# Transpose banks at the start, the last waits, and the semaphores of an RMSNorm and matrix product

## The chip, the core and the metric

The kernel runs on one core of a Trainium2 chip. The time is the device time of one execution in microseconds (us). The core has five engines that run in parallel, each with an instruction stream of its own: TensorE (PE in the profile, with its weight loads as PEld), VectorE (DVE), ScalarE (ACT), GpSimd (POOL) and SyncE (SP). Sixteen DMA engines move data between the device memory (HBM) and the on-chip memory. Engines wait for each other, and for transfers, on semaphores.

## The reference

```python
batch, seq, dim, out_dim = 16, 1024, 512, 768
rms = np.sqrt(np.mean(x ** 2, axis=-1, keepdims=True) + eps)
x_norm = x / rms * gamma
return np.matmul(x_norm, weight).astype(np.float32)
```

There are 16384 rows of 512 numbers. Each is divided by its root mean square, multiplied by `gamma`, and multiplied by a 512 x 768 matrix. Input, weights and output are 32-bit floats: 33.6 MB of x are read and 50.3 MB of output are written.

## The kernel before

The rows are cut into 128 tiles of 128 rows, and two tiles make a pair `j`. The scale by the root mean square is put behind the product, since it is one number per row; `gamma` is multiplied into the weights once, which are kept as bfloat16.

For one tile, GpSimd casts x to bfloat16 (`cast`, L178). Two neighbouring bfloat16 numbers are taken as one 32-bit word, and TensorE turns blocks of 128 x 128 words (`transpose_word`, L216): two words' blocks per tile. They go to one of two PSUM banks, `tp[j % 2]`, so that both tiles of a pair share a bank. VectorE copies them to `xT` (`evac`, L224), for one tile at a time in pairs 0, 1 and 2 (pair 0 by `transpose_tile`, pairs 1 and 2 with `alone=True`) and for a whole pair afterwards. Four weight loads (`hold`, L281) and eight products (`product`, L285) per tile sum up in one of three accumulators `ops`. ScalarE scales the even tile of a pair and VectorE the odd one into the output buffer `ot` (`finish_tile`, `scale`, L264 and L266). ScalarE also computes the squares (L186) and the roots (L191), VectorE the reciprocals (L193). In some pairs VectorE turns the data instead of TensorE (`cast_quad`, `move`, L245 and L256).

SP issues the transfers of x, the weights and the output (L167, L328, L278), all on one queue, in the order in which they stand in the program. x is loaded in groups that begin small (2, 2, 4, 8 tiles), and the output is stored in groups (2, 2, 4, 4, 4, then 8 tiles, and 4 and 4 at the end). `ot` has three buffers of 8 tiles and `xt` two of 16, so a load can be issued when the buffer's tiles have been used.

Nothing is scheduled by a planner: the order on each engine is the order of the calls in the program. The class `Order` records each operation with the cells that it reads and writes, and `emit` then issues all of them and puts in the waits that the cells ask for. For each engine it keeps what the engine is known to have awaited, so that no wait is put in twice. An engine that waits stands still, with all that is queued behind it. In `emit`, an engine that others wait for has one counting semaphore. Each transfer that is awaited has one of its own, and at the end, at L87 and L88, SP waits for those transfers that nobody else awaits: the last four stores.

The recording is emitted within one `tile_critical` section. At its end SP releases a semaphore, each engine answers, SP waits for the answers, and then all engines meet at a barrier, GpSimd clears the program's semaphores in one instruction, and they meet once more.

The start, to which the change goes, is this order on TensorE (`warm_up(n)` is one weight load and `n` products of zeros that nothing uses):

```python
    warm_up(6)
    ...   # gamma is turned and copied, casts 0 to 3, norms 0 and 1
    warm_up(4)
    transpose_tile(0)
    transpose_tile(1)
    warm_up(2)
    weights(0, DVE, 0, WIDE)
```

Of the kernel before, what the change touches and what calls it, by code (L numbers as in the profile page):

```python
# [12 lines left out]
BF16 = mybir.dt.bfloat16  # L13
# [3 lines left out]
P = 128  # L17
# [3 lines left out]
class Order:  # L21
# [4 lines left out]

    def __init__(self, tc):
        self.tc, self.ops = tc, []  # L30

# [6 lines left out]
    def emit(self):  # L38
        nc = self.tc.nc
        streams = {id(e): n for n, e in enumerate((nc.tensor, nc.vector, nc.scalar, nc.gpsimd, nc.sync))}  # L40
        writer, readers = {}, {}
        known = [dict() for _ in streams]
        clocks, needs, place = [], [], []
        count = [0] * len(streams)
        for n, (proc, engine, _, reads, writes) in enumerate(self.ops):
            at = streams[id(engine)]
            if proc is None:
                me, turn = ("transfer", n), 1
            else:
                count[at] += 1  # L50
                me, turn = at, count[at]
            written = {writer[cell] for cell in reads + writes if cell in writer}
            read = {d for cell in writes for d in readers.get(cell, ())}
            need = []
            for d in sorted(written | read, reverse=True):
                who, when = place[d]
                if who == me and (engine is nc.tensor or d not in written):
                    continue
                if known[at].get(who, 0) < when:
                    need.append(d)  # L60
                    for k, v in clocks[d].items():
                        known[at][k] = max(known[at].get(k, 0), v)
            clock = dict(known[at])
            clock[me] = turn
            place.append((me, turn))
            clocks.append(clock)
            needs.append(need)
            for cell in reads:
                readers.setdefault(cell, []).append(n)
            for cell in writes:  # L70
                writer[cell], readers[cell] = n, []
        awaited = {d for need in needs for d in need}
        last = [n for n, (me, _) in enumerate(place) if not isinstance(me, int) and n not in awaited]
        sems, marks, done = {}, {}, {}
        for n in sorted(awaited | set(last)):
            me = place[n][0]
            if me not in sems:
                sems[me] = self.tc.alloc_semaphore(f"done{len(sems)}")
            done[me] = done.get(me, 0) + (1 if isinstance(me, int) else 16)
            marks[n] = (sems[me], done[me])  # L80
        for n, (proc, engine, issue, _, _) in enumerate(self.ops):
            for d in needs[n]:
                engine.wait_ge(*marks[d])
            ins = issue()
            if n in marks:
                ins.then_inc(marks[n][0], 1 if isinstance(place[n][0], int) else 16)
        for n in last:  # L87
            nc.sync.wait_ge(*marks[n])  # L88


@with_exitstack
def kernel(
# [8 lines left out]
    nc = tc.nc  # L101
    PE, DVE, ACT, POOL, SP = nc.tensor, nc.vector, nc.scalar, nc.gpsimd, nc.sync
    order = Order(tc)

    def run(engine, issue, reads=(), writes=()):
        order.add(1, engine, issue, reads, writes)

    x = x.flatten_outer_dims()
    out = out.flatten_outer_dims()
# [5 lines left out]
    XG, OG = 16, 8  # L115
    AHEAD = 20

    def stretches(group, parts):
        first, size, i = {}, {}, 0
        for g in range(NT // group):  # L120
            for n in parts.get(g, [group]):
                for t in range(i, i + n):
                    first[t], size[t] = i, n
                i += n
        return first, size

    last = NT // OG - 1
    x_first, x_size = stretches(XG, {0: [2, 2, 4, 8], **{g: [8, 8] for g in (1, 2, 5, 6, 7)}})
    o_first, o_size = stretches(OG, {0: [2, 2, 4], 1: [4, 4], last: [4, 4]})
# [5 lines left out]
    def sb(name, shape, dtype):  # L135
        return nc.alloc_sbuf_tensor(name, shape, dtype).ap()
# [6 lines left out]
    ident_f = sb("ident_f", [P, P], F32)  # L143
    g_sb = sb("g_sb", [P, 2, 2], F32)
    xt = [sb(f"xt{n}", [P, XG, D], F32) for n in range(2)]
    xb = [sb(f"xb{n}", [P, 8, D], BF16) for n in range(2)]
    jk = [sb(f"jk{n}", [P, D], BF16) for n in range(2)]
    xT = [sb(f"xT{n}", [P, 2, 2, P, 2], BF16) for n in range(4)]
    xq = [sb(f"xq{n}", [P, 4, D], BF16) for n in range(2)]
    xTq = [sb(f"xTq{n}", [P, 4, 2, P, 2], BF16) for n in range(2)]  # L150
    ot = [sb(f"ot{n}", [P, OG, O], F32) for n in range(3)]
    ssq = sb("ssq", [P, NT], F32)
    rms = sb("rms", [P, NT], F32)
    rstd = sb("rstd", [P, NT], F32)
    psum = nc.alloc_psum_tensor("ps", [P, 8 * WIDE], F32).ap()
    ops = [psum[:, 2 * WIDE * n:2 * WIDE * (n + 1)] for n in range(3)]
    tp = [psum[:, WIDE * n:WIDE * (n + 1)].rearrange("p (t h m) -> p t h m", t=2, h=2) for n in (6, 7)]

    def cells(name, slot, i, n=1):
        return [(name, slot, t) for t in range(i, i + n)]  # L160
# [28 lines left out]
    def root(i, n):  # L189
        s = slice(i, i + n)  # L190
        run(ACT, lambda: ACT.activation(out=rms[:, s], in_=ssq[:, s], func=AF.Sqrt, scale=1.0 / D, bias=eps_sb),  # L191
            [("ssq", t) for t in range(i, i + n)] + ["eps"], [("rms", i)])
        run(DVE, lambda: DVE.reciprocal(out=rstd[:, s], in_=rms[:, s]), [("rms", i)],  # L193
            [("rstd", t) for t in range(i, i + n)])

    def norms(i, n):
        for t in range(n):
            square(i + t)
        root(i, n)
# [6 lines left out]
    def norms_of_group(j):  # L206
        square(2 * j)
        square(2 * j + 1)
        if j in norm_end:
            root(*norm_end[j])  # L210

    def transpose_word(j, t, h):
        s = j // 4 % 2
        words = xb[s].rearrange("p a d -> p (a d)").bitcast(F32)
        lo = (j % 4 * 2 + t) * (D // 2) + h * P
        run(PE, lambda: PE.transpose(out=tp[j % 2][:, t, h, :], in_=words[:, lo:lo + P], identity=ident_f),  # L216
            cells("xb", s, j % 4 * 2 + t) + ["ident"], [("tp", j % 2)])

    xT_of = {}

    def evac(j, t=0, n=2):
        src = tp[j % 2].rearrange("p t h m -> p t (h m)").bitcast(BF16)
        dst = xT[j % 4].rearrange("p t h m c -> p t (h m c)")
        run(DVE, lambda: DVE.tensor_copy(out=dst[:, t:t + n, :], in_=src[:, t:t + n, :]),  # L224
            [("tp", j % 2)], cells("xT", j % 4, t, n))
        for a in range(t, t + n):
            xT_of[2 * j + a] = (xT[j % 4][:, a], ("xT", j % 4, a))

    def transpose_tile(i):
        for h in range(2):  # L230
            transpose_word(i // 2, i % 2, h)
        evac(i // 2, i % 2, 1)
# [29 lines left out]
    def scale(engine, dst, src, r, reads, writes):  # L262
        if engine is ACT:
            run(ACT, lambda: ACT.mul(out=dst, in_=src, mul=r), reads, writes)  # L264
        else:
            run(DVE, lambda: DVE.tensor_single_scalar(out=dst, in_=src, scalar=r, op=mybir.AluOpType.mult), reads, writes)  # L266
# [3 lines left out]
    def accumulator():  # L270
        return next(turns) % 3

    def store(i):
        first, n = o_first[i], o_size[i]
        s = first // OG % 3
        if i == first + n - 1:
            src = ot[s][:, first % OG:first % OG + n, :]
            order.transfer(SP, lambda: SP.dma_start(out=rows(out, first, n), in_=src), reads=cells("ot", s, first % OG, n))  # L278

    def hold(lhsT, cell):  # L280
        run(PE, lambda: PE.ldweights(lhsT), [cell])  # L281

    def product(dst, lhsT, rhs, start, stop, reads, writes):

        run(PE, lambda: PE.add_instruction(mybir.InstMatmult(  # L285
            name=nc.get_next_instruction_name(), engine=mybir.EngineType.PE,
            ins=[PE.lower_ap(rhs), PE.lower_ap(lhsT)], outs=[PE.lower_ap(dst)],
            start_tensor_calc=start, stop_tensor_calc=stop, tile_size=(P, P), tile_position=(0, 0), ldweights=False)),
            reads, writes)
# [11 lines left out]

    def finish_tile(i, a, engine):
        s = i // OG % 3
        scale(engine, ot[s][:, i % OG, :], ops[a][:, :O], rstd[:, i:i + 1],
              [("ops", a, 0), ("ops", a, 1), ("rstd", i)], [("ot", s, i % OG)])
        store(i)

    def feeder(pairs, gaps, alone=False):
# [34 lines left out]
    def warm_up(n):  # L343
        hold(warm[:, :P], "warm")
        for _ in range(n):
            product(ops[spare][:, :WIDE], warm[:, :P], warm, True, True, ["warm"], [("ops", spare, 0)])
# [15 lines left out]
    cast(1)  # L362
    cast(2, 2)
    norms(0, 2)
    warm_up(4)
    transpose_tile(0)
    transpose_tile(1)
    warm_up(2)
# [9 lines left out]
    cast(4, 2)  # L378
    matmuls(0, acc[0], [2, 3])
    finish_tile(0, acc[0], ACT)  # L380
    matmuls(1, acc[1], [2, 3], feeder([1], [2, 2], alone=True))
    finish_tile(1, acc[1], DVE)
    cast(6, 2)

# [3 lines left out]
    for j in range(1, NP):  # L388
# [23 lines left out]
        for i, engine in ((2 * j, ACT), (2 * j + 1, DVE)):  # L412
            a = accumulator()
# [1 line left out]
            finish_tile(i, a, engine)  # L415

    with tc.tile_critical():  # L417
        order.emit()


# [33 lines left out]
```

## Time and profile before

| | |
|---|---|
| median of 4 runs | 210.38 us (210.01 to 211.48) |
| profiled execution | 211.72 us, span 209.7 us |
| PE busy | 196.2 us, 94% of the span |
| VectorE, ScalarE, GpSimd busy | 149.5, 144.4, 59.9 us |
| DMA | 85.62 MB, mean 408 GB/s |
| granted TensorE clock, mean | 0.981 |
| chain that ended last, by engine | PE 75%, DMA 11%, VectorE 6% |

The span runs from the first to the last instruction of the profiled execution; the time of that execution has some 2.0 us more around it. A row of a timeline has the start and the length in us, the engine, the line and the operation, and in brackets the idle time of the engine just before and what ended it. Rows of the same kind that follow each other are merged (x2).

### The profile page before, as it was taken

The numbers are of one execution on the slowest core, as the hardware profiler recorded it, in microseconds if no ns is written. First come the engines' busy times: TensorE is split into PE (matmuls) and PEld (weight loads), VectorE is DVE, ScalarE is ACT, GpSimd is POOL, SyncE is SP. The second block draws the span as 40 slices with busy tenths as digits, with TensorE's granted clock in tenths as the row PEclk, the third lists the DMA queues.
The fourth block names the chain that finished last, engine by engine and source line by source line (L and its number), as shares of the span: only waits on it lengthen the run. The fifth ranks groups of instructions, "written<-read, shape, count | busy, mean of one in ns | idle before, by whom it ended". The sixth has DMA issues, their size and how long they took to land.

```text
span 209.7 us, 2788 instructions
## 1 busy us (share of the span) xinstructions
PE 196.2 (94%) x1238; PEld 73.0 (35%) x717; DVE 149.5 (71%) x255; ACT 144.4 (69%) x343; POOL 59.9 (29%) x34
## 2 busy tenths in 40 slices
PE   7899999999999999998999999999999999999900
PEld 0234433442443334432333334443334334333200
DVE  0446557998589957997579966998589967998310
ACT  4688897877768696756877686877778596853300
POOL 3147633036300390005700670025500372000000
PEclk9999999999999999999999999999999999999975
DMA  6999999999999999999999999999999999987992
GB/s 233 405 447 422 347 408 436 430 436 429 434 447 413 428 439 422 459 397 433 420 422 431 449 422 420 433 419 419 425 430 422 431 438 434 441 356 309 410 417 120
DMA packets 5488, 85.62 MB, mean 408 GB/s; under 512 B 610, under 2 KB 612, under 8 KB 1380
## 3 DMA queue, kind: packets, MB, share of 16 engines
q1 hardware_dynamic: 5472, 85.46, 96.5%
q8 instruction: 7, 0.11, 0.2%
q14 instruction: 5, 0.04, 0.0%
q10 hardware_dynamic: 4, 0.00, 0.0%
HBM read 35.13 MB, written 50.33 MB: 408 GB/s over the span
## 4 chain that ended last, share of the span: by engine, by line
PE 75%; DMA 11%; DVE 6%; issue 1%; ACT 1%; SPq 0%; DVEq 0%; ACTq 0%
PE ps L285 66%; DMA xt<-in_x_dram 11%; PE ps L216 9%; DVE ot L266 2%; DVE xTq L256 2%; DVE xT L224 2%; ACT jk L186 0%; ACT ot L264 0%; DVE w_bf L266 0%; SPq L278 0%; PE ps L354 0%; DVE warm L336 0%; DVE rstd L193 0%; DVEq L449 0%; DVE eps_sb L337 0%
## 5 line engine op out<-in xcount | busy, mean ns | idle before, releaser
L285 PE MATMUL ps<-w_bf,xT 128*128 128x512 bf16 (+1 forms) x800 | 148.3, 327 | 0.7 <-ACT ot L264 0.6
L264 ACT ACTIVATE ot<-ps,rstd 128x768 f32<-128x768 f32 x64 | 57.5, 898 | 43.1 <-PE ps L285 40.2
L186 ACT ACTIVATE jk<-xt 128x512 bf16<-128x512 f32 x128 | 78.7, 619 | 7.3 <-DMA xt<-in_x_dram 7.3
L178 POOL CAST xb<-xt 128x2048 bf16<-128x2048 f32 (+3 forms) x21 | 46.3, 2218 | 113.7 <-DMA xt<-in_x_dram 97.9
L266 DVE TENSOR_SCALAR ot<-ps,rstd 128x768 f32<-128x768 f32 x64 | 64.8, 1013 | 9.3 <-PE ps L285 8.6
L281 PEld LDWEIGHTS <-xT 128*128 128x128 bf16 x400 | 39.4, 98 | 60.1 <-issue 53.2
L216 PE MATMUL ps<-ident_f,xb 128*128 128x128 f32 x200 | 54.5, 276 | 0.7 <-DVE xT L224 0.7
L224 DVE COPY xT<-ps 128x1024 bf16<-128x1024 bf16 (+1 forms) x53 | 34.7, 654 | 27.1 <-PE ps L216 25.4
L256 DVE STREAM_TRANSPOSE xTq<-xq 32x256 f32<-32x256 f32 x112 | 48.7, 435 | 3.4
L216 PEld LDWEIGHTS ps<-ident_f,xb 128*128 128x128 f32 x200 | 28.3, 143 | 46.9 <-issue 43.4
L285 PE MATMUL ps<-w_bf,xTq 128*128 128x512 bf16 x224 | 42.8, 326 | 0.0
L186 ACT ACTIVATION_READ_ACCUMULATOR jk<-xt 128x1 f32 x128 | 24.3, 190 | 0.0
L281 PEld LDWEIGHTS <-xTq 128*128 128x128 bf16 x112 | 11.0, 98 | 14.5 <-issue 14.5
L245 POOL CAST xq<-xt 128x2048 bf16<-128x2048 f32 x7 | 13.3, 1894 | 0.0
L193 DVE RECIPROCAL rstd<-rms 128x8 f32<-128x8 f32 (+3 forms) x20 | 3.8, 192 | 6.6 <-ACT rms L191 6.3
L285 PE MATMUL ps<-warm 128*128 128x512 bf16 x12 | 5.7, 630 | 1.4 <-DVE eps_sb L337 1.4
L191 ACT ACTIVATE rms<-ssq,eps_sb 128x8 f32<-128x8 f32 (+3 forms) x20 | 6.0, 300 | 0.6
L264 ACT ACTIVATE w_bf<-w_f,g_sb 128x768 bf16<-128x768 f32 x2 | 1.9, 934 | 1.7 <-DMA w_f<-in_weight_dram 1.7
L360 DVE COPY g_sb<-ps 128x4 f32<-128x4 f32 x1 | 0.2, 163 | 3.2 <-PE ps L354 3.2
L324 ACT ACT_TABLE_LOAD x1 | 1.3, 1283 | 1.5 <-SPq L417 1.5
L266 DVE TENSOR_SCALAR w_bf<-w_f,g_sb 128x512 bf16<-128x512 f32 (+2 forms) x3 | 1.3, 481 | 0.0
L354 PEld LDWEIGHTS ps<-ident_f,g_row 2*128 2x128 f32 x2 | 0.3, 202 | 2.6 <-issue 2.6
(10 smaller groups left out, 2.0 us busy)
## 6 DMA issues: line engine op xcount, KB each, us to landing
out_dram<-ot SPq DMA_DIRECT2D x13, 3072.0 KB, 17.5
xt<-in_x_dram SPq DMA_DIRECT2D x11, 2048.0 KB, 19.7
xt<-in_x_dram SPq DMA_DIRECT2D x2, 4096.0 KB, 22.7
out_dram<-ot SPq DMA_DIRECT2D x5, 1536.0 KB, 9.8
w_f<-in_weight_dram SPq DMA_DIRECT2D x2, 768.0 KB, 5.8
out_dram<-ot SPq DMA_DIRECT2D x2, 768.0 KB, 15.8
xt<-in_x_dram SPq DMA_DIRECT2D x2, 512.0 KB, 5.4
xt<-in_x_dram SPq DMA_DIRECT2D x1, 1024.0 KB, 9.3
```

The source lines that it names most:

```text
L178: run(POOL, lambda: POOL.tensor_copy(out=xb[s][:, i % 8:i % 8 + n, :], in_=src), of, cells("xb", s, i % 8, n))
L186: run(ACT, lambda: ACT.activation(out=jk[j], in_=src[:, 0, :], func=AF.Square, accum_out=ssq[:, i:i + 1]), of, [("jk", j), ("ssq", i)])
L191: run(ACT, lambda: ACT.activation(out=rms[:, s], in_=ssq[:, s], func=AF.Sqrt, scale=1.0 / D, bias=eps_sb), [("ssq", t) for t in range(i, i ...
L193: run(DVE, lambda: DVE.reciprocal(out=rstd[:, s], in_=rms[:, s]), [("rms", i)], [("rstd", t) for t in range(i, i + n)])
L216: run(PE, lambda: PE.transpose(out=tp[j % 2][:, t, h, :], in_=words[:, lo:lo + P], identity=ident_f), cells("xb", s, j % 4 * 2 + t) + ["id ...
L224: run(DVE, lambda: DVE.tensor_copy(out=dst[:, t:t + n, :], in_=src[:, t:t + n, :]), [("tp", j % 2)], cells("xT", j % 4, t, n))
L245: run(POOL, lambda: POOL.tensor_copy(out=xq[s], in_=src), of, [("xq", s)])
L256: run(DVE, lambda: DVE.transpose(out=dst, in_=src), [("xq", s)], [("xTq", s)])
L264: run(ACT, lambda: ACT.mul(out=dst, in_=src, mul=r), reads, writes)
L266: run(DVE, lambda: DVE.tensor_single_scalar(out=dst, in_=src, scalar=r, op=mybir.AluOpType.mult), reads, writes)
L281: run(PE, lambda: PE.ldweights(lhsT), [cell])
L285: run(PE, lambda: PE.add_instruction(mybir.InstMatmult(name=nc.get_next_instruction_name(), engine=mybir.EngineType.PE, ins=[PE.lower_ap(r ...
```

## The change

Four things are changed.

The tiles 0 to 5 (pairs 0 to 2) are transposed into alternating banks: the second tile of a pair goes into the other bank than the first. From pair 3 on, a pair has one bank as before. The second warm-up before the first transposes has two products in place of four.

The waits for the last four stores are no longer emitted in the section of the recording, but in a second `tile_critical` section that holds nothing else. The other engines have no work in it.

A transfer takes over the semaphore of an earlier transfer if the engine that issues it is already known to have awaited that one, directly or through others. Otherwise it gets a new one. The program has 13 semaphores of its own in place of 43.

The scale of the last tile of each output group also waits for the scale of the tile before it. The store then needs to wait for one engine alone.

```diff
@@ emit
+            if proc is None:
+                free = [k for k, d in enumerate(slots) if known[at].get(("transfer", d), 0)]
+                if free:
+                    slots[free[0]] = n
+                else:
+                    slots.append(n)
+                slot_of[n] = ("slot", slots.index(n))
...
-        for n in sorted(awaited | set(last)):
-            me = place[n][0]
-            if me not in sems:
-                sems[me] = self.tc.alloc_semaphore(f"done{len(sems)}")
-            done[me] = done.get(me, 0) + (1 if isinstance(me, int) else 16)
-            marks[n] = (sems[me], done[me])
+        for n in range(len(self.ops)):
+            me = slot_of.get(n, place[n][0])
+            if n in slot_of or n in awaited:
+                if me not in sems:
+                    sems[me] = self.tc.alloc_semaphore(f"done{len(sems)}")
+                done[me] = done.get(me, 0) + (16 if n in slot_of else 1)
+                marks[n] = (sems[me], done[me])
...
-        for n in last:
-            nc.sync.wait_ge(*marks[n])
+        return [marks[n] for n in last]
@@ transposes
+    def bank(j, t):
+
+        return (j + t) % 2 if j < 3 else j % 2
+
     def transpose_word(j, t, h):
-        s = j // 4 % 2
+        s, b = j // 4 % 2, bank(j, t)
...
-        run(PE, lambda: PE.transpose(out=tp[j % 2][:, t, h, :], in_=words[:, lo:lo + P], identity=ident_f),
-            cells("xb", s, j % 4 * 2 + t) + ["ident"], [("tp", j % 2)])
+        run(PE, lambda: PE.transpose(out=tp[b][:, t, h, :], in_=words[:, lo:lo + P], identity=ident_f),
+            cells("xb", s, j % 4 * 2 + t) + ["ident"], [("tp", b)])
@@ finish_tile
+        before = [("ot", s, i % OG - 1)] if i == o_first[i] + o_size[i] - 1 else []
         scale(engine, ot[s][:, i % OG, :], ops[a][:, :O], rstd[:, i:i + 1],
-              [("ops", a, 0), ("ops", a, 1), ("rstd", i)], [("ot", s, i % OG)])
+              [("ops", a, 0), ("ops", a, 1), ("rstd", i)] + before, [("ot", s, i % OG)])
@@ start
-    warm_up(4)
+    warm_up(2)
     transpose_tile(0)
@@ end
     with tc.tile_critical():
-        order.emit()
+        left = order.emit()
+
+    with tc.tile_critical():
+        for sem, count in left:
+            SP.wait_ge(sem, count)
```

`evac` reads from the bank that `bank(j, t)` names, in the same way.

## The prediction

> **What bounds the kernel now.** I read the page's slices first, because two resources are close to full.
>
> ```profile
> DMA  6999999999999999999999999999999999987992
> GB/s 233 405 447 422 347 408 436 430 436 429 434 447 413 428 439 422 459 397 433 420 422 431 449 422 420 433 419 419 425 430 422 431 438 434 441 356 309 410 417 120
> q1 hardware_dynamic: 5472, 85.46, 96.5%
> ```
>
> The second line is the bytes moved in each fortieth of the span (5.24 us). From the second slice to the 35th the 16 DMA engines are busy 9 tenths or more of the time at some 425 GB/s, and one queue, SP's, carries 85.46 MB of it. The PE row of the page is as full (196.2 us of 209.7). So next: which of the two waits for the other. All waits of PE in the execution:
>
> ```profile
> PE ps L285 <- DVE eps_sb L337: 1.4, 1, 1.4
> PE ps L216 <- DVE xT L224: 0.7, 2, 0.5
> PE ps L285 <- ACT ot L264: 0.6, 1, 0.6
> ```
>
> PE waits 2.7 us in all: 1.4 at the start, 0.7 in two waits for the PSUM bank (L216 on L224), 0.6 once for an accumulator. That last one is worth following, on ACT's timeline:
>
> ```profile
> 96.45 0.63 ACT L186 ACTIVATE jk<-xt 128x512 bf16<-128x512 f32 x1 [2.94 <-DMA xt<-in_x_dram]
> 97.69 0.88 ACT L264 ACTIVATE ot<-ps,rstd 128x768 f32<-128x768 f32 x1
> ```
>
> The accumulator's scale (97.69) stood behind ACT's squares, which sat 2.94 us idle for a load of x. So at 98 us PE was limited by the transfers and not the other way round. The last stage, by windows (busy time of each engine, then clock, DMA share and GB/s):
>
> ```profile
> 187.50:191.00 3.50, 3.50 (x24) 1.19 (x12) 3.30 (x7) 1.38 (x2) 0.00 (x0) 1.00 0.38 162
> 191.00:200.00 9.00, 7.96 (x50) 2.25 (x23) 5.13 (x7) 2.70 (x3) 0.00 (x0) 1.00 1.02 433
> 200.00:206.00 6.00, 0.00 (x0) 0.00 (x0) 0.02 (x1) 0.00 (x0) 0.00 (x0) 0.65 0.94 397
> ```
>
> Between 187.5 and 191 the DMA share drops to 0.38: most engines had emptied their queue and waited for the store of tiles 112 to 119, which SP issued at 190.29. From 191 on the share is 1.02 and 0.94 and it stays so past PE's end (199.0): the three last stores, 6.29 MB, follow each other without a gap, so the end is set by when that first one could start plus its queue, about 15.5 us. The packet records add one thing. The 16 engines do not finish together: the last store's 16 completions arrive at 206.21 to 206.56 for 15 of them and at 208.06 for one. That engine finished its share of the preceding store at 191.89, when the others had already started the new one (191.12 to 191.64), and it had no idle time since 2 us; it was 1.5 us behind the 15th at the load that landed at 29.46, and between 0.1 and 1.5 from there on. SP's waits for the last two stores and the clearing of the semaphores at the end:
>
> ```profile
> SPq L88 <- DMA out_dram<-ot: 7.7, 2, 4.1
> ```
>
> ```profile
> L449 POOLq EVENT_SEMAPHORE_RANGE_CLEAR  x1: 308/308/308, 209.1 to 209.1; - x1
> ```
>
> **The change part by part.** The profiled execution took 211.72 us, its span 209.7, with 2.0 around it; it is 1.3 above the median of 210.38, so I make the sums as differences and carry them to the median.
>
> The front, on the merged timeline (start, length, operation, idle time before and its releaser):
>
> ```profile
> 4.40 1.89 PE L285 MATMUL ps<-warm 128*128 128x512 bf16 x4
> 6.00 0.17 DVE L193 RECIPROCAL rstd<-rms 128x2 f32<-128x2 f32 x1 [1.33 <-ACT rms L191]
> 6.75 0.42 DVE L224 COPY xT<-ps 128x512 bf16<-128x512 bf16 x1 [0.59 <-PE ps L216]
> 7.23 0.69 PE L216 MATMUL ps<-ident_f,xb 128*128 128x128 f32 x2 [0.52 <-DVE xT L224]
> 8.30 1.27 DVE L266 TENSOR_SCALAR w_bf<-w_f,g_sb 128x512 bf16<-128x512 f32 x3
> 8.83 3.33 PE L285 MATMUL ps<-w_bf,xT 128*128 128x512 bf16 x14
> 17.28 3.73 POOL L178 CAST xb<-xt 128x2048 bf16<-128x2048 f32 x2 [2.87 <-DMA xt<-in_x_dram]
> ```
>
> *Two warm-up products fewer.* Four took 1.82 us in the chain (4.47 to 6.29), so two are 0.91. Tile 0's transposes move from 6.29 to 5.38; their input, the first of two casts of L178 that start at 4.33 and take 1.16, is ready at 4.91. They take 0.44, to 5.82.
>
> *Tile 1 in a bank of its own.* Its transposes waited 0.52 for tile 0's copy; now they follow at once, 5.82 to 6.26 (cast ready at 5.49). What is late next is VectorE: its reciprocal (6.00 to 6.17, waiting for ACT's root) stands ahead of the copies. So copies at 6.2 and 6.65, done at 7.08; then the first weight scale, 0.41, to 7.5. The first product of tile 0 starts at about 7.55 in place of 8.83: 1.3 us earlier. Of the 0.91 + 0.52 = 1.43, the reciprocal keeps 0.1.
>
> *How much of the 1.3 lives on.* Three loads bound it, and the change moves none of them. The products run at half pace first (weight loads 0.64 us apart up to 10.49, 0.32 after 10.91), so a start 1.3 us earlier is worth 0.65 at full pace, and the bank wait of tile 3 gives 0.19: some 0.85. Tiles 4 and 5 are cast at 12.39 to 13.4, right after their load; PE asked for them at 14.14, so no more than 0.7 is left. Tiles 8 to 11 are the first of the two casts at 17.28, ready at 17.28 + 1.87 = 19.15; PE came to them at 19.65. So 0.5 is left at 20 us, and a new wait of some 0.3 stands on PE there. From there to 98 us PE has no other wait. At 98.6 it waited 0.6 for the landing; if that landing stays, the whole 0.5 turns into waiting there. The queue had never run dry before 188 us, the order of transfers is the same, so a landing does not come earlier because a store is issued earlier. In an execution where that landing is a little earlier than here, some of the 0.5 passes. Bounds for the front at the end: 0 and -0.5; I take -0.2, nearer to the row at 98.6.
>
> *The other banks.* Tiles 2 to 5 alternate too. Pair 3 (tiles 6 and 7, bank 1) now follows tile 5 in bank 1: its first word, at 16.61, needs tile 5's copy, which ended at 16.58. Both move together, so 0, at most 0.1 in PE time that the wait at 19 us covers.
>
> *VectorE awaits ScalarE before a store's last tile.* The 20 scales concerned stood at 0.40 to 1.27 us after the end of the ScalarE scale that they now wait for, so the wait is met: 0. If it were not, the VectorE copy of the next pair (L224) would queue behind it, and PE behind that. SP has one wait fewer at each store; VectorE's was the one that came last, so 0.
>
> *Shared semaphores.* Transfers wait for nothing new: a semaphore is taken over only when its engine already knows the transfer to be over. 49 semaphores are cleared at the end now, 19 later. The clearing took 0.308 us, and in the trace the 49 updates are 5.4 ns apart: 30 x 5.4 ns = -0.16.
>
> *The second section.* Now, from the landing (208.08) SP goes through a wait, a branch (0.16), a release that all engines answer, and two more waits, and reaches the final barrier at 208.73: 0.65. Afterwards the others have answered before, while the stores fly, but SP has three more wait instructions behind the landing (0.065 each by the row spacing at 208.48 to 208.61) and a release, drain and no-op of its own: 0.2 + 0.07 + 0.16 + 0.09 + 0.08 + 0.13 = 0.73. So +0.08, with bounds -0.3 (the answers gone, the added waits free) and +0.3 (each added step costing as much as the branch).
>
> Sum: -0.2 - 0.16 + 0.08 = -0.28, so 210.38 - 0.28 = 210.1 us, and 211.4 for an execution like the profiled one. By the bounds: -0.5 - 0.16 - 0.3 = -0.96 and 0 - 0.16 + 0.3 = +0.14.
>
> A rule that speaks against taking warm-up away: the half pace ended at about 10.7 us here, 3.4 us after the restart at 7.23. In the Trainium skill, "TensorE: Matmul & The Clock Gate", Part 1, the clock is released by a busy window of about 3.4 us that runs freely, whatever starts in it, so the release varies from run to run. The trace agrees with the length; that it runs freely no run here shows. By the row, PE is idle only 7.1 to 7.55 after the change, so the release stays near 10.7 and costs 0; by the page it could come a window later in some runs, which would add at most what the slower rival below gives.
>
> **The rivals.** *Nothing of the front arrives.* The one late DMA engine sets the end, and it had no idle time: then only the tail's -0.08 is left, 210.3. For it: the landing at 208.06, 1.5 us after the 15th. Against it: the timed runs are 1.3 us shorter than the profiled one, so that engine may lag less in them.
>
> *The front gain arrives whole (faster).* The loads land earlier in unprofiled runs than here, so that PE keeps the 1.3 us, or 0.85 and a shorter tail (-0.3): 210.38 - 1.3 - 0.08 = 209.0. Against it: the cast at 17.28 had to wait 2.87 us for its load, and that load would have to land 0.8 us earlier. It decides where the x loads of tiles 8 to 15 land before 16.4 us.
>
> *The clock rises a window later (slower).* If the shorter warm-up makes PE miss the busy window, 3.4 us run at 0.64 for 0.32 and 1.7 us are lost, at the front. The cover: 0.5 at the cast of tiles 8 to 11, and the wait of 0.6 at 98.6 where there is one. So +0.6 to +1.2 is left, 211.0 to 211.6. For it: the idle 0.45 us at 7.1; against: PE was more idle (6.73 to 7.23) just ahead of the window that released the clock here. It decides once the loss is over 1.1 us.
>
> **How the numbers follow.** The forecast (a loss or gain of a few tenths) has 0.60, the rival of nothing arriving 0.12, the faster one 0.18, the slower one 0.10. The first two lie within 0.5% (1.05 us, about what a measurement of this kernel tells from no change: its four runs spread over 1.47 us), but for 0.02 of the forecast's low end. So faster 0.20, same 0.70, slower 0.10. The range takes the forecast's bounds (209.4 to 210.5), half a spread of the runs above, 0.7, and reaches down towards the faster case: 209.1 to 211.2.
>
> **What would show it.** Right: the first product near 7.6 us; no wait of tile 1's transposes on the copy of tile 0; a new PE wait near 19 us for the cast; the wait near 98 us longer by some 0.4 or the same; the DMA rows as before; the clearing at about 0.15 us. Wrong: PE's end earlier by a microsecond or more, weight loads 0.64 us apart beyond 11 us, or more than 1 us from the last landing to the final barrier.

## The result, and the profile after

The median is 209.82 us (209.51 to 212.08, 47 runs) against 210.27 us for the kernel before (78 runs beside them), a ratio of 0.9981 with a 95% interval of 0.9974 to 0.9988. That is 0.45 us by the medians and 0.25 to 0.55 us by the interval of the ratio. 210.1 had been forecast, a gain of 0.28.

The profiled execution took 209.82 us, its span 207.9. Its transfers, by slices of 5.2 us, look like before: the 16 DMA engines are at 9 tenths or more from the second slice to the 36th, and 85.62 MB are moved.

```profile
DMA  6999999999999999999999999999999999995995
```

All waits of PE:

```profile
PE ps L298 <- DVE eps_sb L352: 1.4, 1, 1.4
PE ps L298 <- DVE w_bf L279: 1.0, 2, 0.8
PE ps L298 <- ACT ot L277: 0.9, 2, 0.7
PE ps L228 <- POOL xb L186: 0.9, 2, 0.6
```

The waits for the bank are gone. In their place stand waits for the weights (1.0) and for casts (0.9). The wait for the accumulator near 98 us has not gone, it is 0.7 us there. ScalarE's timeline around it shows the same cause as before, the squares wait for a load of x:

```profile
96.14 0.63 ACT L194 ACTIVATE jk<-xt 128x512 bf16<-128x512 f32 x1 [3.02 <-DMA xt<-in_x_dram]
97.38 0.88 ACT L277 ACTIVATE ot<-ps,rstd 128x768 f32<-128x768 f32 x1
```

The start and the places where the front's gain ends, from the merged timeline:

```profile
4.41 0.74 PE L298 MATMUL ps<-warm 128*128 128x512 bf16 x2
4.98 0.90 PE L228 MATMUL ps<-ident_f,xb 128*128 128x128 f32 x4
5.97 0.73 DVE L237 COPY xT<-ps 128x512 bf16<-128x512 bf16 x2
7.16 1.51 PE L298 MATMUL ps<-w_bf,xT 128*128 128x512 bf16 x8 [0.84 <-DVE w_bf L279]
10.58 0.44 PE L228 MATMUL ps<-ident_f,xb 128*128 128x128 f32 x2 [0.60 <-POOL xb L186]
11.97 2.03 POOL L186 CAST xb<-xt 128x1024 bf16<-128x1024 f32 x2 [1.44 <-DMA xt<-in_x_dram]
13.16 0.30 PE L228 MATMUL ps<-ident_f,xb 128*128 128x128 f32 x1 [0.32 <-POOL xb L186]
16.86 3.74 POOL L186 CAST xb<-xt 128x2048 bf16<-128x2048 f32 x2 [2.86 <-DMA xt<-in_x_dram]
18.81 0.33 PE L228 MATMUL ps<-ident_f,xb 128*128 128x128 f32 x1
```

The first product starts at 7.16 us (8.83 before). The two waits for casts stand at tile 2 (10.58, 0.60 us) and at tile 4 (13.16, 0.32 us), whose cast is the first of the two that begin at 11.97, right after their load. At tile 8 (18.81), where the prediction looked for a new wait, the row has none: TensorE comes there just as the first of the two casts that begin at 16.86 ends. The windows at the end (busy times, clock, DMA share, GB/s):

```profile
187.50:191.00 3.50, 3.50 (x23) 1.19 (x12) 3.30 (x7) 1.07 (x2) 0.00 (x0) 1.00 0.53 225
191.00:200.00 9.00, 7.65 (x48) 2.16 (x22) 4.87 (x6) 2.70 (x3) 0.00 (x0) 1.00 0.94 399
200.00:206.00 6.00, 0.00 (x0) 0.00 (x0) 0.00 (x0) 0.00 (x0) 0.00 (x0) 0.72 0.93 393
```

From 187.5 to 191 us the engines are half idle again (0.53), then the three last stores fill the queue. SP's wait for them, now in the second section, and the clearing:

```profile
SPq L468 <- DMA out_dram<-ot: 5.9, 1, 5.9
```

```profile
L468 POOLq EVENT_SEMAPHORE_RANGE_CLEAR  x1: 138/138/138, 207.5 to 207.5; - x1
```

The clearing takes 0.138 us in place of 0.308. From the last landing to the end of the span it is 1.41 us, 1.61 before.

What was not expected is in the next table, which has the runs of the sections below too. In every trace the first of the 16 engines lands its share of the last store 15.9 us after the issue of the store of tiles 112 to 119. That store goes out 0.03 us after the scale of tile 119, so in the kernels with all of TensorE's work the early engines follow TensorE. The last engine lands 0.03 to 1.9 us behind the 14th.

| profiled execution | store of 112 to 119 issued | PE end | last store lands: 1st, 14th, 16th engine | landing to end of span |
|---|---|---|---|---|
| before | 190.29 | 198.96 | 206.21, 206.36, 208.06 | 1.61 |
| changed | 189.97 | 198.65 | 205.91, 206.06, 206.48 | 1.41 |
| front only | 189.81 | 198.49 | 205.74, 205.90, 206.33 | 1.60 |
| section only | 189.27 | 197.94 | 205.20, 205.36, 206.51 | 1.63 |
| semaphores only | 190.79 | 199.47 | 206.72, 206.83, 206.89 | 1.40 |
| front undone | 189.77 | 198.43 | 205.69, 205.85, 206.23 | 1.41 |
| front delayed | 190.51 | 199.19 | 206.44, 206.55, 206.60 | 1.41 |
| changed again | 189.79 | 198.46 | 205.72, 205.87, 206.67 | 1.41 |
| split loads | 188.61 | 197.28 | 204.53, 205.26, 207.01 | 1.41 |
| fewer instructions | 188.24 | 193.93 | 204.17, 205.05, 206.66 | 1.41 |
| narrow products | 187.98 | 194.95 | 203.88, 205.14, 207.01 | 1.42 |
| split loads, less stored | 189.68 | 198.35 | 205.62, 205.73, 205.76 | 1.41 |
| the same, front undone | 188.74 | 197.41 | 204.68, 204.79, 204.82 | 1.41 |

In the eleven executions that store everything the first landing moves by 2.8 us (203.88 to 206.72), and the last one does not follow it: it stays between 206.23 and 208.06. When the store goes out early, one engine or a few are still behind with the store before it (in the changed kernel that one lands its last share at 191.82, 1.85 us after the issue), and they end the execution. When it goes out late (semaphores only, front delayed: 190.79 and 190.51), all 16 land within 0.17 us, and the end follows the store. So the end is the later of two, the queue's and TensorE's, and in this kernel they lie close together.

### The profile page after: what moved, and what is told of

Same layout as the page of the kernel before. It is cut to its first block, busy times and chain, and to the rows that moved or that the text cites. A ratio compares the mean times of both kernels' runs of the same rounds, so it can differ in the third digit from the quotient of the medians.

```text
span 207.9 us, 2784 instructions
## 1 busy us (share of the span) xinstructions
PE 194.2 (93%) x1236; PEld 72.3 (35%) x717; DVE 149.3 (72%) x255; ACT 144.6 (70%) x343; POOL 59.9 (29%) x34
## 2 busy tenths in 40 slices
DMA packets 5488, 85.62 MB, mean 412 GB/s; under 512 B 610, under 2 KB 612, under 8 KB 1380
## 4 chain that ended last, share of the span: by engine, by line
PE 71%; DMA 16%; DVE 5%; issue 1%; SPq 1%; ACT 1%; POOL 1%; ACTq 0%
PE ps L298 63%; DMA xt<-in_x_dram 16%; PE ps L228 8%; DVE ot L279 2%; DVE xTq L269 2%; DVE xT L237 1%; POOL xb L186 1%; ACT jk L194 0%; SPq L343 0%; SPq L175 0%; ACT ot L277 0%; SPq L291 0%; DVE rstd L201 0%; SPq L468 0%; ACTq L92 0%
## 5 line engine op out<-in xcount | busy, mean ns | idle before, releaser
L279 DVE TENSOR_SCALAR ot<-ps,rstd 128x768 f32<-128x768 f32 x64 | 64.8, 1013 | 9.7 <-PE ps L298 9.1
L298 PE MATMUL ps<-warm 128*128 128x512 bf16 x10 | 4.1, 544 | 1.4 <-DVE eps_sb L352 1.4
L279 DVE TENSOR_SCALAR w_bf<-w_f,g_sb 128x512 bf16<-128x512 f32 (+2 forms) x3 | 1.4, 482 | 0.8 <-DMA w_f<-in_weight_dram 0.8
```

Of the source, the lines that this page charges most:

```text
L298: run(PE, lambda: PE.add_instruction(mybir.InstMatmult(name=nc.get_next_instruction_name(), engine=mybir.EngineType.PE, ins=[PE.lower_ap(r ...
```

## The experiments

Two theories stood at the start. A: the front's gain is covered by waits for transfers, and what is measured comes from the shorter clearing. B: the front's gain passes to the end.

### Each part alone

The front alone, in the kernel before:

```diff
+    def bank(j, t):
+        return (j + t) % 2 if j < 3 else j % 2
...
-    warm_up(4)
+    warm_up(2)
     transpose_tile(0)
```

> The kernel before with the front of the change alone: alternating banks for tiles 0 to 5 and two warm-up products fewer. Theory A (cover): TensorE comes some 0.5 us earlier to tile 8, waits there for the cast, and the rest is given back at 98 us, where it waits for ScalarE, whose squares wait for a load; PE wait near 98 us 0.6 to 1.1 us, time 0 to 0.15 us below the kernel before. Rival B (the front passes): the time falls by 0.3 to 0.5 us, most of the 0.45 measured for the whole change.

The ratio to the kernel before is 1.0 (0.9987 to 1.0013), 210.25 us. PE's first product came at 7.20, and the wait near 98 us was 0.7 us. B falls: the least that it asked for, 0.3 us, is a ratio of 0.9986, just outside the interval.

The second section alone:

```diff
-        for n in last:
-            nc.sync.wait_ge(*marks[n])
+        return [marks[n] for n in last]
...
-        order.emit()
+        left = order.emit()
+
+    with tc.tile_critical():
+        for sem, count in left:
+            SP.wait_ge(sem, count)
```

> The kernel before with the second section for the last waits alone; 43 semaphores of its own as before. Theory A: from the last landing to the final barrier 0.65 us before and 0.63 in the changed kernel, so the time stays within 0.1 us. Rival C (the answers of the engines cost more than the trace shows): 0.2 to 0.3 us below the kernel before.

1.0 (0.9987 to 1.0012). SP reached the final barrier 0.68 us after the last landing, against 0.67 before and 0.66 in the changed kernel: the answers that are gone and the waits that came in are equal. The interval alone, 0.3 us wide to each side, would leave room for C's 0.2 us; the trace does not. The clearing was as long as before:

```profile
L452 POOLq EVENT_SEMAPHORE_RANGE_CLEAR  x1: 308/308/308, 207.5 to 207.5; - x1
```

The shared semaphores alone, the last waits in the first section:

```diff
+            if proc is None:
+                free = [k for k, d in enumerate(slots) if known[at].get(("transfer", d), 0)]
...
+        for n in last:
+            nc.sync.wait_ge(*marks[n])
```

> The kernel before with shared semaphores alone, 13 in place of 43; the last waits stay in the first section. Theory A: the clearing at the end takes 0.14 us in place of 0.31, the step after it is as long, so 0.15 to 0.25 us below the kernel before. Rival B (the front passes): less than 0.1 us of the change is here. The DMA rows as before in both.

0.9996 (0.9984 to 1.0008). The interval holds the 0.2 us of the trace (0.9990), and it holds no gain at all as well. The trace itself is plain, and all profiled executions with shared semaphores agree on it (1.40 to 1.42 us from landing to end, against 1.60 to 1.63 in the three without):

```profile
L457 POOLq EVENT_SEMAPHORE_RANGE_CLEAR  x1: 138/138/138, 207.9 to 207.9; - x1
```

The fourth part, the scale that waits for the scale before it, was not run alone. In all thirteen traces, with it and without it, each of the 20 stores is issued 0.03 us after the last scale of its group, so at the stores it changes nothing.

### Is it TensorE that the end waits for?

The loads of tiles 48 to 79 split, in the changed kernel, to take away the wait near 98 us:

```diff
-    x_first, x_size = stretches(XG, {0: [2, 2, 4, 8], **{g: [8, 8] for g in (1, 2, 5, 6, 7)}})
+    x_first, x_size = stretches(XG, {0: [2, 2, 4, 8], **{g: [8, 8] for g in range(1, 8)}})
```

> The changed kernel, with the loads of tiles 48 to 63 and 64 to 79 split into two of 8 tiles each, as the other groups are. Theory A: the first half lands earlier, so PE's wait of 0.7 us near 98 us goes, PE ends up to 0.7 us earlier, and the store of tiles 112 to 119 is issued earlier; 14 or 15 DMA engines stood idle then, so the time falls by 0.2 to 0.6 us against the changed kernel (0.65 to 1.05 against the kernel before). Rival D (one late DMA engine sets the end whatever PE does): the wait goes and the time stays within 0.1 us of the changed kernel. Rival E: the wait moves to another load, time the same.

1.0 (0.9988 to 1.0012), 210.04 us: no faster than the changed kernel, and by the medians 0.2 us slower. PE's waits in it, all of them, and two of the windows:

```profile
PE ps L298 <- DVE eps_sb L352: 1.4, 1, 1.4
PE ps L228 <- POOL xb L186: 0.9, 2, 0.6
PE ps L298 <- DVE w_bf L279: 0.4, 1, 0.4
```

```profile
187.50:191.00 3.50, 3.50 (x24) 1.07 (x11) 3.34 (x6) 1.08 (x2) 0.00 (x0) 1.00 0.78 330
200.00:206.00 6.00, 0.00 (x0) 0.00 (x0) 0.00 (x0) 0.00 (x0) 0.00 (x0) 0.59 0.73 309
```

The wait near 98 us is gone, PE ended at 197.28, 1.37 us earlier, and the store went out 1.36 us earlier. The DMA share from 187.5 to 191 rose from 0.53 to 0.78. Fourteen engines landed by 205.26, the last at 207.01. A falls: TensorE was earlier by more than was asked, and the time did not follow. Of the three, D fits the trace, one or two late engines end this execution; its 0.1 us was missed, for the time rose by 0.2. E falls too, the wait has not moved to another load.

The front undone in the changed kernel:

```diff
-        return (j + t) % 2 if j < 3 else j % 2
+        return j % 2
...
-    warm_up(2)
+    warm_up(4)
     transpose_tile(0)
```

> The changed kernel with its front as before: one bank per pair and four warm-up products. Theory D (the transfers set the end): the end does not follow TensorE, so the time is that of the changed kernel within 0.15 us, 0.1 to 0.45 below the kernel before, and PE's wait near 98 us is shorter by the 0.3 to 0.5 us that it starts later. Rival B (the front passes): the time goes back by 0.3 us or more, to the kernel before.

0.9985 (0.9970 to 1.0000), where the changed kernel beside it has 0.9984. No gain of the front is seen, though the two intervals, 0.3 us wide to each side, would hide some tenths of it. The expected shorter wait at 98 us did not come (0.7 again), and the timeline says why:

```profile
11.91 2.03 POOL L186 CAST xb<-xt 128x1024 bf16<-128x1024 f32 x2 [1.44 <-DMA xt<-in_x_dram]
13.01 0.33 PE L228 MATMUL ps<-ident_f,xb 128*128 128x128 f32 x1
16.82 3.73 POOL L186 CAST xb<-xt 128x2048 bf16<-128x2048 f32 x2 [2.88 <-DMA xt<-in_x_dram]
18.76 0.33 PE L228 MATMUL ps<-ident_f,xb 128*128 128x128 f32 x1
```

The first product came at 8.41 here, 1.25 us later than in the changed kernel. But tile 4's transposes start 1.10 us after their cast does, against 1.19 in the changed kernel, which had waited 0.60 and 0.32 us for casts by then. Tile 8's transposes start 1.94 us after the cast at 16.82, against 1.95. With the old front TensorE is at these casts in time as well, so the front's gain has ended at 13 us, and no part of it reached 98. In the profiled execution of the kernel before, tile 8's transposes came 2.37 us after the cast's start. There TensorE left its half pace late, at 10.67 us; in the four others with the old front (section only, semaphores only, this one, and the last run below) it did so at 4.04 to 6.22.

The front delayed, six products in the second warm-up of the changed kernel in place of two:

```diff
-    warm_up(2)
+    warm_up(6)
     transpose_tile(0)
```

> The changed kernel with six in place of two products in the second warm-up, 0.9 us (full pace) to 1.8 us (half pace) more ahead of the first product. Theory D: the wait at the cast of tiles 8 to 11 and the wait near 98 us shrink or go, PE's end moves by less than 0.6 us, and the time stays within 0.2 us of the changed kernel. Rival B: 0.5 to 1.5 us above the changed kernel.

0.9986 (0.9971 to 1.0000): the time of the changed kernel. The first product came at 7.90, the waits for the weights (1.0), the casts (0.9) and near 98 us (0.7) were as long as in the changed kernel. In that execution the first loads landed some 0.9 us later (the cast of tiles 8 to 11 began at 17.80), and PE followed them. So the trace does not show a delay against the loads; that it costs nothing rests on the twelve timed executions.

The changed kernel once more, on the same chip:

> The changed kernel once more, beside the other three on the same chip, since its three parts, each alone, moved the time by less than 0.1 us. Theory A: what is left is the shorter clearing, so 0.1 to 0.25 us below the kernel before. Rival G (the parts need each other): 0.35 to 0.55 below again.

0.9984 (0.9970 to 0.9999), 209.93 against 210.17 us. Theory A asked for 0.1 to 0.25 us; it is 0.24 by the medians and 0.34 by the ratio (0.02 to 0.63). A is enough, but the interval holds G's 0.35 to 0.55 as well, so G stays open.

### The queue, and what waits for it

Split loads, and 1.57 MB less to store:

```diff
         if i == first + n - 1:
+            n = 4 if first == 72 else n
```

> The changed kernel with the split loads of the run before, and it leaves out the store of tiles 76 to 79: 1.57 MB less, which is 3.7 us of the queue at 425 GB/s. Theory D: the queue is what the split kernel waited for at the end, so all engines are idle when the store of tiles 112 to 119 is issued (188.6 us), the 16 last landings come within 0.5 us of each other, near 205.0, and the time falls by 1.2 to 2.0 us against the split kernel, to 208.0 to 208.9. Rival F (the end is bound by TensorE and the last stores alone): the time stays at 210.0, since neither has changed.

0.9902 (0.9879 to 0.9926), 208.29 us, 1.75 below the split kernel by the medians. The windows show why: the engines are mostly idle before the last stores go out.

```profile
184.00:187.50 3.50, 3.50 (x26) 1.43 (x14) 3.33 (x8) 1.77 (x3) 0.00 (x0) 1.00 0.35 147
187.50:191.00 3.50, 3.50 (x24) 1.04 (x11) 3.34 (x6) 0.90 (x1) 0.00 (x0) 1.00 0.26 112
```

The 16 last landings came at 205.62 to 205.76. That profiled execution was the slowest of seven (209.13 us), with its first loads late by 0.9 us again, so its landings are later than the 205.0 expected. F falls: with fewer bytes the time falls, and TensorE's work is the same. Of the 3.7 us of the queue only 1.75 were gained: all 16 landings now follow the store of tiles 112 to 119 by 15.9 to 16.1 us, so the end is TensorE's here.

The same with the front undone, by the diff of the run above that undid it:

> The run with split loads that leaves out the store of tiles 76 to 79, now with the front as before (one bank per pair, four warm-up products). Theory D: with the waits for transfers gone, TensorE's start passes to the end, so the time is 0.3 to 0.8 us above that run (208.6 to 209.1). Rival I (the front is worth nothing in any case): within 0.15 us of that run, 208.3.

208.32 us, 0.9918 (0.9905 to 0.9931), against 208.29 and 0.9902 on another chip. By the medians that is nothing, by the ratios 0.3 us with intervals as wide, so the times alone do not decide between I and the least that D asked for. The traces decide for I. Tile 8's transposes start 1.95 us after their cast without the change's front and 1.94 with it, and from the start of that cast to PE's end it is 180.53 and 180.52 us: even with the transfers eased at the end, nothing of the front is left behind that cast.

Then TensorE taken out of the way. First with fewer instructions:

```diff
-            hold(lhsT, cell)
-            for half, lo, hi in ((0, 0, WIDE), (1, WIDE, O)):
-                product(ops[a][:, lo:hi], lhsT, w_bf[:, k, lo:hi], k == 0, k == K - 1,
+            if k == 0:
+                hold(lhsT, cell)
+            for half, lo, hi in ((0, 0, WIDE), (1, WIDE, O)) if k == 0 else ():
+                product(ops[a][:, lo:hi], lhsT, w_bf[:, k, lo:hi], k == 0, True,
```

> The changed kernel, leaving out the weight loads and products of three of the four blocks of 128 features (TensorE has some 1150 of its 1741 instructions fewer). All transfers are as before. Theory D: TensorE is out of the way, the store of tiles 112 to 119 is issued before the queue is empty, and the end is the queue's alone: 204 to 207 for the last landing, 207.5 to 209.9 us in all, so much less than TensorE's saving of some 120 us. Theory H (the late engine carries the instruction loads): 16 KB instruction loads fall from 7 to 2 or 3, the 16 last landings spread over less than half of what they do in the run with narrow products.

And with all of them, but narrow:

```diff
-            for half, lo, hi in ((0, 0, WIDE), (1, WIDE, O)):
+            for half, lo, hi in ((0, 0, WIDE), (1, WIDE, O)) if k == 0 else ((0, 0, 64), (1, WIDE, WIDE + 64)):
```

> The changed kernel, leaving out columns: in three of the four blocks of features the products take 64 columns in place of 512 and 256. TensorE has as many instructions as in the changed kernel, and less than half of its work. Theory D: the queue alone sets the end, 204.5 to 207 for the last landing, so 208 to 210 us in all. Theory H: seven instruction loads of 16 KB as in the changed kernel, and the last landing of the 16 engines comes 2 us or more after the eighth, 0.5 us or more later than in the run with fewer instructions.

209.91 us (0.9994, 0.9981 to 1.0006) and 210.44 us (1.0015, 1.0006 to 1.0024), a little above the ranges that were expected (209.9 and 210). More than half of the columns that TensorE multiplies are left out, its busy time falls from 194.2 to 112.0 and 127.3 us, and the time of the kernel is the same or a little more. This is the plainest answer: with TensorE out of the way nothing is gained, so the kernel's time is that of its transfers. What PE, and then ScalarE, waited for with fewer instructions:

```profile
PE ps L298 <- DVE ot L279: 38.7, 34, 2.4
PE ps L298 <- ACT ot L277: 31.6, 22, 5.6
```

```profile
ACT jk L194 <- DMA xt<-in_x_dram: 30.3, 8, 7.9
ACT ot L277 <- DMA out_dram<-ot: 7.9, 3, 3.5
```

PE waited for the accumulators' scales, and ScalarE, in its turn, for loads (30.3 us) and for the stores that free its output buffer (7.9). This is also why the store of tiles 112 to 119 goes out only 1.7 and 2.0 us earlier than in the changed kernel: the chain that leads to it runs through a store that lands at 177.5 and 177.3 us and frees the output buffer. With narrow products the queue has hardly a gap at the end, where the changed kernel had 0.53:

```profile
187.50:191.00 3.50, 1.23 (x17) 0.64 (x8) 3.32 (x7) 0.90 (x1) 0.00 (x0) 0.86 0.92 393
```

Theory H got no support as it was put. The 16 KB instruction loads fell from 7 to 3, as expected, but the last engine landed 2.4 us after the eighth, and 3.0 us with all instructions: less, but not by half. The last landing itself came 0.35 us later with all instructions, where 0.5 or more was expected. The 0.5 us between the two medians goes the way that H says. Which work makes an engine late stays open.

## Why the prediction was right, point by point

- *The bound.* "The one late DMA engine sets the end" was put as a rival with 0.12, and the forecast let some of the front pass. The runs show that the end does not come earlier with TensorE, as the rival had it: with split loads PE ended 1.37 us earlier and the time did not fall; with more than half of its columns left out it did not fall; with 1.57 MB less it fell by 1.75 us. The rival is not the whole account either, for in two executions the store went out late and all 16 engines followed it. One reading was off: the late engine finished its share of the store before at 192.82 and not at 191.89.
- *The front at the start.* 7.55 us was predicted for the first product, it was 7.16. Here the clock had risen at 4.72 us, so the transposes and the products ran at full pace.
- *What lives on of it.* This is the step that was mis-sized. The prediction left 0.5 us at 20 us, from the row of tile 8's transposes at 19.65, and took 0.2 for the end. That loads bound the front was right, but the casts that did it were those of tiles 2 to 5, at 10.58 and 13.16 us, and not that of tiles 8 to 11. With the front undone, tile 4's and tile 8's transposes stand as long after their casts as in the changed kernel (1.10 and 1.94 us against 1.19 and 1.95): 0 is left at 13 us, and none is seen at the end (0.9985 against 0.9984). The 0.5 was the lag of the one profiled execution, whose clock rose late, and not the lag of the old front.
- *The wait at 98 us.* It was said to grow by 0.4 or stay the same. It was 0.7 for 0.6, and 0.7 with the front undone, so it does not tell the fronts apart.
- *Banks of pair 3, VectorE's wait for ScalarE.* Costed at nothing; the changed trace shows no wait of a transpose for a copy, and no wait of L279 for ScalarE among VectorE's longest.
- *The clearing.* 30 x 5.4 ns = 0.16 was predicted, 0.308 - 0.138 = 0.17 was found.
- *The second section.* +0.08 was predicted within -0.3 and +0.3. Landing to barrier took 0.67 us before (0.65 in the prediction, which counts from SP's row at 208.08) and 0.66 after: 0.
- *The faster rival.* It needed the load of tiles 8 to 15 before 16.4 us. Their cast began at 16.70 us or later in all thirteen traces, so its case did not come up.
- *The slower rival.* The clock did not rise later with less warm-up. It rose at 4.72 to 6.76 us in five executions with the new front, and at 4.04 to 10.67 in five with the old. The page "TensorE: Matmul & The Clock Gate" of the Trainium skill (Part 1) has it that the window runs freely; these times, for the same order of work, agree with it. A first product that came 1.25 us later (front undone) cost nothing; the 1.7 us of this rival were not tried.

So the sum came to -0.28 by a front of -0.2 that is not there, a clearing that is, and +0.08 that is not. Of the measured 0.25 to 0.55 us the traces account for 0.2 (landing to end 1.41 for 1.61). For the rest the three parts alone (1.0, 1.0 and 0.9996, each to 0.0013) show no place; it is within what these intervals leave, and it stays open. That the forecast lay so close is partly luck: one of its three terms was found, and it alone is 0.16 of the 0.28.

## What to carry to other kernels

When two resources are both at 94% or more, look below the mean: here it showed the 16 DMA engines half idle at 187 us, while in most executions one or two of them were still behind and set the end. To find out what the end waits for, take out half of one resource's work and see whether the time moves; that told more than the parts of the change one by one. And a gain at the start has to be followed to the first place where the engine waits for something that the change does not move, in more than one execution, since one trace may hold a late clock or a late load.

## What the runs showed of the hardware

- The 16 DMA engines of one queue drift apart: in the changed kernel the 16 shares of the last store landed within 0.57 us, with split loads within 2.48, before within 1.85. A transfer is over when the last of them is: in the changed kernel the 16th landed at 206.48, and SP's wait ended at 206.50.
- TensorE's half pace ended between 4.04 and 10.67 us in executions that begin alike. By PE's end nothing of it was left: from the start of the cast of tiles 8 to 11 it is 181.68 us before (10.67), 181.61 with the front undone (6.22) and 181.79 in the changed kernel (4.72).
- Clearing 49 semaphores took 0.308 us and clearing 19 took 0.138, a difference of 5.7 ns for each.
- The first loads landed up to 1.1 us later in some executions (the cast of tiles 8 to 11 began at 16.70 to 17.83 us), with the same order of issue.
